# Attention probabilities left undivided until the values leave PSUM, in a hybrid attention and MLP layer

## The chip, the core and the metric

The kernel runs on one core of a Trainium2 chip. The core has five engines that run side by side, each through its own queue of instructions, in order: PE (TensorE, matmuls), ACT (ScalarE), DVE (VectorE), POOL (GpSimd) and SP (SyncE, which here issues every DMA). Matmuls write into PSUM, a memory of eight banks of 128 partitions x 512 f32; everything else lies in SBUF. The metric is device time in microseconds (us).

## What is computed

One layer on 1024 positions of 1024 features. A normalised and modulated x is projected; the columns of the projection feed two groups of eight attention heads, and their outputs go through one output projection; a gated MLP with a short convolution follows. The change concerns only the softmax of the attention heads:

```python
# MLA heads: dense, causal by chunks of 64
s = einsum('bqhd,bkhd->bhqk', q, k) * scale
p = softmax(where(mask, s, NEG_INF))
o = einsum('bhqk,bkhd->bqhd', p, v)
...
# chunk heads: a band of 9 chunks of keys, with a bias by relative position
s = einsum('bqhd,bkhd->bhqk', q, k_band) * scale + bias
p = softmax(where(valid, s, NEG_INF))
o = einsum('bhqk,bkhd->bqhd', p, v_band)
```

## The kernel before

**Stages.** A start (modulation vectors, normalisation, transposes, the first projection) fills the first 95 us. Then the attention runs as one interleaved stream. Its pieces are *units*: one head and one half (g) of the queries, 16 units of chunk attention (names with c) and then 16 of MLA (names with m). A unit has four *tiles* of 128 queries; tile i of a chunk head sees the last five blocks of 128 keys at most, tile i of an MLA head sees i+1 blocks. So a tile's scores are 128 x n with n from 128 to 640 (chunk) or to 1024 (MLA).

**A tile's scores** (`Unit.scores`, L636). PE multiplies the q page by the k pages (L658; each f32 operand is split in a high and a low part, three products for each block) into a two-buffered PSUM tile "S". DVE masks (L665, L676) and takes the row minimum m of the negated scores (L669, L673 or L677). ACT computes exp(m - s) into P and the row sum beside it (L683). DVE takes the reciprocal of the sum and multiplies it by 2^15 (L685, L686): ri, a column of 128. Then the row is split into two f16 halves in "hl": POOL writes the high half, P x ri rounded to f16 (L71, called from L700; all modes are "1"), and DVE writes the low half, P x ri minus the high half (L703). Rows of more than 640 columns go in two pieces, so there are 64 pieces in chunk attention and 88 in MLA. A transposing DMA on SP's queue (L705) turns hl into "PT", keys on partitions. P, hl and PT have three buffers each.

**A tile's values** (`Unit.values`, L709). PE multiplies PT by the f16 values, high and low halves side by side (L716), into the PSUM tile "pv" of the unit, one bank, one buffer. After the fourth tile ACT copies one half of the partitions with a scale (L723), DVE adds the other half, scaled (L724), and SP sends the 64 x 512 result to memory (L725). The scale is a power of two from `pow2_scale` (L337), which also takes the 2^15 out again (L351).

**What sets the order.** The main loop (L817) issues a tile's scores, and values three tiles (DEPTH) later. After each, `pace` takes steps of *fillers*, the projections that the later units need: f_v, f_qk and f_m during chunk attention, f_up (the MLA up-projections; much of it on POOL: L116, L467 to L470, L582) at the change to MLA, and f_oca (part of the output projection, L598 to L611) during MLA. f_ada (L419) streams weights beside them. On top of that a list scheduler orders each engine's queue by priorities: scores may move ahead by 400, the split and transposes by 200, values by 200 (OFF_S, OFF_P, OFF_V). Before a unit starts, its q and k pages are made (`qk_page`, L614): four PE transposes (L618) into a PSUM tile with the tag "T", evicted by ACT (L621 or L624) and DVE (L622 or L625). The tag T has one buffer (TB = 1), one bank; the latents (L496) use it too.

**After the attention** (from about 678 us) come the rest of the output projection, the second normalisation and the MLP. They share no line with the change.

Of the kernel before, what the change touches and what calls it, by code (L numbers as in the profile page):

```python
# [12 lines left out]
F32 = mybir.dt.float32  # L13
# [4 lines left out]
AF = mybir.ActivationFunctionType  # L18
# [3 lines left out]
MUL, ADD, SUB, MIN, MAX = ALU.mult, ALU.add, ALU.subtract, ALU.min, ALU.max  # L22

P = 128
# [14 lines left out]
DEPTH = 3  # L39
OFF_S, OFF_P, OFF_V = 400, 200, 200  # L40
P_BUFS, HL_BUFS, PT_BUFS, TB = 3, 3, 3, 1
MODE_C = "1111"
MODE_M = "1111"
PSCALE, VSCALE = 2.0 ** 15, 2.0 ** 14
R_CA, R_MLA = 1.9, 0.5


# [15 lines left out]
def layer_kernel(ctx, tc, I, out):  # L63
    nc = tc.nc
    pe, act, dve, pool, sp = nc.tensor, nc.scalar, nc.vector, nc.gpsimd, nc.sync
# [4 lines left out]
    def scale_pool(o, i, s):  # L70
        pool.tensor_scalar(o, i, s, 1.0, op0=MUL, op1=MUL)  # L71
# [12 lines left out]
    cst = ctx.enter_context(tc.tile_pool(name="cst", bufs=1))  # L84
# [11 lines left out]
    ident = cst.tile([P, P], F32, name="ident")  # L96
# [33 lines left out]
    ps = psA.__enter__()  # L130
# [105 lines left out]
    for d in range(ND):  # L236
        if d + 1 < ND:
            load_ada(d + 1)
        w = wada[d]
# [15 lines left out]
        for t in range(NT):  # L255
            h, j = divmod(t, 4)
# [80 lines left out]
    def pow2_scale(nm, ssw, b2, n, fac):  # L337
        t = cst.tile([P, 3, ND], F32, name=f"vs{nm}")
        dve.tensor_tensor(t[:, 0, :n], ssw, b2, op=MUL)
        pt = ps.tile([P, 512], F32, name=f"vsp{nm}", tag="mm", bufs=2)  # L340
        pe.matmul(pt[:, :n], ones[:], t[:, 0, :n], start=True, stop=True)
        dve.tensor_reduce(t[:, 1, 0:1], pt[:, :n], axis=AX.X, op=ADD)
        dve.tensor_scalar(t[:, 1, 0:1], t[:, 1, 0:1], fac, 1e-30, op0=MUL, op1=ADD)
        pool.tensor_tensor(t[:, 1, 1:2], t[:, 1, 0:1], nhalf[:], op=ALU.pow)
        ab = cst.tile([P, 2], F32, name=f"vab{nm}")
        dve.tensor_scalar(t[:, 2, 0:1].bitcast(I32), t[:, 1, 1:2].bitcast(I32), 0x7F800000, None, op0=ALU.bitwise_and)
        dve.reciprocal(t[:, 2, 1:2], t[:, 2, 0:1])
        dve.tensor_scalar(t[:, 2, 1:2], t[:, 2, 1:2], 1.0001, None, op0=MUL)
        dve.tensor_scalar(t[:, 2, 1:2].bitcast(I32), t[:, 2, 1:2].bitcast(I32), 0x7F800000, None, op0=ALU.bitwise_and)
        dve.tensor_scalar(ab[:, 0:1], t[:, 2, 0:1], VSCALE, None, op0=MUL)  # L350
        dve.tensor_scalar(ab[:, 1:2], t[:, 2, 1:2], 1.0 / (VSCALE * PSCALE), None, op0=MUL)  # L351
        return ab[:, 0:1], ab[:, 1:2]

    hb = cst.tile([P, ND], F32, name="hb")
# [273 lines left out]
    class Unit:  # L628
# [7 lines left out]
        def scores(u, i):  # L636

            qpg, kpgs = u.pages()
            bias = u.bias() if u.band else None
            lo = max(0, i - 4) if u.band else 0  # L640
            n = (i - lo + 1) * P
            nm = f"{u.nm}_{i}"
            rsum = cst.tile([P, 1], F32, name=f"rs{nm}", tag="rsum", bufs=4)
            ri = cst.tile([P, 1], F32, name=f"ri{nm}", tag="ri", bufs=4)
            with tc.high_priority(offset=OFF_S):
                s = ps.tile([P, 1024], F32, name=f"s{nm}", tag="S", bufs=2)
                n0 = max(0, min(4, i + 1) - lo) * P
                n1 = n - n0
                c0 = 512 - n0 if n1 else 0
                segs = [(c0, lo * P, n0, 0)] if n0 else []  # L650
                if n1:
                    segs.append((512, max(lo, 4) * P - 512, n1, 1))
                q = slice((i % 4) * P, (i % 4 + 1) * P)
                rs_ = slice(u.base, u.base + u.rows)
                for a in range(2):
                    for c, ko, w, kh in segs:
                        for b in range(2 - a):
                            last = pe.matmul(s[:, c:c + w], qpg[rs_, a, q], kpgs[kh][rs_, b, ko:ko + w],  # L658
                                             start=(a == 0 and b == 0), stop=(a == 1))
                trail.append(last.ins)  # L660
                sv = s[:, c0:c0 + n]
                m = cst.tile([P, 1], F32, name=f"m{nm}", tag="m", bufs=4)
                if u.band:
                    if i >= 4:
                        dve.memset(sv[64:128, 0:64], BIG)  # L665
                    w = min(n, 256)
                    if n > 256:
                        m0 = cst.tile([P, 1], F32, name=f"m0{nm}", tag="m0", bufs=4)
                        dve.tensor_reduce(m0[:], sv[:, :n - 256], axis=AX.X, op=MIN)  # L669
                        init = m0[:]  # L670
                    else:
                        init = 3e38
                    dve.tensor_tensor_reduce(sv[:, n - w:n], sv[:, n - w:n], bias[:, 256 - w:256], 1.0, init,  # L673
                                             ADD, MIN, accum_out=m[:])
                else:
                    dve.memset(sv[0:64, n - 64:n], BIG)  # L676
                    dve.tensor_reduce(m[:], sv, axis=AX.X, op=MIN)  # L677
                pieces = [(0, n)] if n <= 640 else [(0, 512), (512, n)]
                if n <= 640:
                    pr = at.tile([P, 640], F32, name=f"P{nm}", tag="P", bufs=P_BUFS)  # L680
                else:
                    pr = pgtile([P, 1024], F32, f"P{nm}")
                act.activation(pr[:, :n], sv, AF.Exp, bias=m[:], scale=-1.0, accum_out=rsum[:, 0:1])  # L683
            with tc.high_priority(offset=OFF_P):
                dve.reciprocal(ri[:], rsum[:, 0:1])  # L685
                dve.tensor_scalar(ri[:], ri[:], PSCALE, None, op0=MUL)  # L686
                u.pt[i] = []
                for x, (p0, p1) in enumerate(pieces):
                    w = p1 - p0
                    hl = at.tile([P, 1280], F16, name=f"hl{nm}_{x}", tag="HL", bufs=HL_BUFS)  # L690
                    pp = pr[:, p0:p1]
                    cnt[0] += 1
                    mode = (MODE_C if u.band else MODE_M)[cnt[0] % 4]
                    if mode == "2":
                        scale_pool(pp, pp, ri[:])
                        act.activation(hl[:, :w], pp, AF.Copy)
                        pool.tensor_tensor(hl[:, w:2 * w], pp, hl[:, :w], op=SUB)
                    else:
                        if mode == "1":
                            scale_pool(hl[:, :w], pp, ri[:])  # L700
                        else:
                            act.activation(hl[:, :w], pp, AF.Copy, scale=ri[:])
                        dve.scalar_tensor_tensor(hl[:, w:2 * w], pp, ri[:], hl[:, :w], op0=MUL, op1=SUB)  # L703
                    tt = at.tile([P, 10, P], F16, name=f"PT{nm}_{x}", tag="PT", bufs=PT_BUFS)
                    sp.dma_start_transpose(tt[:, :2 * w // P, :], hl[:, :2 * w])  # L705
                    u.pt[i].append((tt, lo + p0 // P, w // P))
            return sum(3 * max(107, w / 2.4) for _, _, w, _ in segs)

        def values(u, i):  # L709
            if i % 4 == 0:  # L710
                u.pv = ps.tile([P, 512], F32, name=f"pv{u.nm}_{u.g}", tag="pv", bufs=1)
            c = slice((i % 4) * P, (i % 4 + 1) * P)
            todo = [(lo + j, tt[:, h * nk + j, :]) for tt, lo, nk in u.pt[i] for j in range(nk) for h in range(2)]
            with tc.high_priority(offset=OFF_V):
                for x, (j, mov) in enumerate(todo):
                    last = pe.matmul(u.pv[:, c], u.vst(j), mov, start=(x == 0), stop=(x == len(todo) - 1))  # L716
                trail.append(last.ins)
                if i % 4 == 3:
                    sb = at.tile([P, 512], F32, name=f"sb{u.nm}_{u.g}", tag="sb", bufs=1)
                    dst = at.tile([P, 512], F32, name=f"o{u.nm}_{u.g}", tag="o", bufs=1)  # L720
                    r0, r1 = (slice(64, 128), slice(0, 64)) if u.odd else (slice(0, 64), slice(64, 128))
                    inv = vscale[u.vs][1]
                    act.activation(sb[r0], u.pv[r1], AF.Copy, scale=inv[r1])  # L723
                    dve.scalar_tensor_tensor(dst[r0], u.pv[r0], inv[r0], sb[r0], op0=MUL, op1=ADD)  # L724
                    sp.dma_start(u.dst_d[r0, u.g * 512:(u.g + 1) * 512], dst[r0])  # L725
            return 56 * len(todo)

    cnt = [0]
    biases = {}

    def load_bias(hd):
# [85 lines left out]
    for n in range(len(tiles) + DEPTH):  # L817
        if n < len(tiles):
            u, i = tiles[n]
# [4 lines left out]
        if n >= DEPTH:  # L824
            u, i = tiles[n - DEPTH]
# [326 lines left out]
```

## Time and profile before

| | us |
|---|---|
| median of 3 runs (1463.65 to 1468.99) | 1465.47 |
| the profiled execution | 1464.36 |
| its span, first to last instruction | 1462.2 |
| PE busy over the span | 1278.0 |
| DVE | 1013.6 |
| POOL | 823.0 |
| ACT | 611.4 |

The table of the page gives for each engine its busy time, the share of the span and the number of instructions. PEld is the loading of weights into PE, which overlaps the matmuls. Matmuls are pipelined, and the ends of their records are modelled: the records of neighbours overlap. A row of a group reads: line, engine, operation, what it writes <- what it reads, shapes, xcount | busy us, mean ns of one | idle time of the engine just before, and what ended that wait. A row of waits reads: who waited <- for whom: us in total, times, the longest. PEclk is the clock that was granted to PE, as a share of the full one.

### The profile page before, as it was taken

Reading aid. Unit: us, or ns where it says so; the run is one execution under the profiler, and the core shown is the slowest. Engines: PE = TensorE matmul, PEld = TensorE weight load, DVE = VectorE, ACT = ScalarE, POOL = GpSimd, SP = SyncE. Lnnn points to the kernel's source line nnn. Section 1 sums busy time; section 2 is a strip of 40 time slices with the busy share of each in tenths; the row PEclk is TensorE's granted clock in tenths of the full one; section 3 lists DMA queues with packets and bytes.
Section 4 is the critical chain, followed back from the end, with each engine's and each line's share of the span. In section 5 each row is a group of like instructions: output and inputs, shape, how many; then the busy total and the mean of one; then the engine's idle time right before and its main releaser. Section 6 shows DMA issues by size and latency. Waiting matters only on the chain.

```text
span 1462.2 us, 20198 instructions
## 1 busy us (share of the span) xinstructions
PE 1278.0 (87%) x6836; PEld 1058.7 (72%) x6836; DVE 1013.6 (69%) x1734; ACT 611.4 (42%) x1190; POOL 823.0 (56%) x845
## 2 busy tenths in 40 slices
PE   3859989998967788885776999999999998999997
PEld 2759878886756666664655878788888887887885
DVE  6874776476667868872476887777777777566653
ACT  4453354243455545543274434344444433332331
POOL 5263554274599954534644555566655555665662
PEclk9979987999787899996887999999999999999998
DMA  7323647455522577879611322322222244446442
GB/s 281 134 71 74 131 114 148 129 119 120 112 52 51 115 163 156 180 142 253 246 72 59 105 110 101 116 87 87 87 87 83 75 140 164 151 144 238 146 142 101
DMA packets 218595, 185.94 MB, mean 127 GB/s; under 512 B 148086, under 2 KB 183034, under 8 KB 217468
## 3 DMA queue, kind: packets, MB, share of 16 engines
q1 hardware_dynamic: 218492, 184.66, 44.5%
q8 instruction: 54, 0.88, 0.3%
q14 instruction: 49, 0.40, 0.1%
HBM read 121.17 MB, written 28.84 MB: 103 GB/s over the span
## 4 chain that ended last, share of the span: by engine, by line
PE 39%; DMA 17%; DVE 15%; POOL 13%; issue 12%; ACT 3%; SPq 1%; DVEq 0%; POOLq 0%; ACTq 0%
POOL wds L82 5%; DMA aw<-w_ada 5%; PE p L924 4%; PE p L926 4%; PE p L925 4%; DMA wu<-w_up 3%; DMA PTm<-hlm 3%; PE sc L658 2%; PE dnp L1067 2%; PE dnp L1069 2%; PE dnp L1068 2%; PE sm L658 2%; DVE adacc L243 2%; DVE aacc L430 1%; DVE u L1002 1%
## 5 line engine op out<-in xcount | busy, mean ns | idle before, releaser
L82 POOL TENSOR_TENSOR wds<-wd,wds 128x512 fp32r<-128x512 f32 x88 | 154.6, 1777 | 99.0 <-ACT wds L75 99.0
L82 POOL TENSOR_TENSOR wc<-ws,wc 128x512 fp32r<-128x512 f32 x22 | 65.4, 2972 | 137.8 <-ACT wc L75 137.8
L1057 DVE TENSOR_TENSOR wd<-wd,gmbc 128x1024 f32<-128x1024 f32 x44 | 67.5, 1533 | 80.4 <-DMA wd<-w_down 80.4
L1069 PE MATMUL dnp<-wds,g 128*128 128x512 f32 x308 | 118.4, 390 | 4.5 <-DVE g L82 4.5
L1067 PE MATMUL dnp<-wds,g 128*128 128x512 f32 x308 | 119.6, 390 | 1.9 <-DVE xo L1075 1.9
L75 ACT ACTIVATE wds<-wd 128x512 fp32r<-128x512 f32 x88 | 54.8, 624 | 157.3 <-PE dnp L1069 152.2
L1068 PE MATMUL dnp<-wds,g 128*128 128x512 f32 x308 | 119.5, 389 | 0.0
L71 POOL TENSOR_SCALAR hlm<-Pm,rim 128x512 f16<-128x512 f32 (+4 forms) x88 | 61.9, 706 | 70.1 <-DMA PTm<-hlm 55.1
L703 DVE SCALAR_TENSOR_TENSOR hlm<-Pm,rim,hlm 128x512 f16<-128x512 f32 (+4 forms) x88 | 68.0, 777 | 30.1 <-POOL hlm L71 29.7
L71 POOL TENSOR_SCALAR hlc<-Pc,ric 128x640 f16<-128x640 f32 (+2 forms) x64 | 45.3, 710 | 76.9 <-DVE ric L686 41.2
L1015 DVE TENSOR_TENSOR ws<-wu,wu 128x512 f32<-128x512 f32 x22 | 30.7, 1396 | 76.2 <-DMA wu<-w_up 76.2
L82 DVE TENSOR_TENSOR g<-gr,g 128x512 fp32r<-128x512 f32 x44 | 71.9, 1635 | 11.5 <-ACT g L75 11.5
L1001 DVE SCALAR_TENSOR_TENSOR u<-c,pk,u 128x1023 f32<-128x1023 f32 x44 | 77.4, 1765 | 2.0 <-ACT u L1000 2.0
L1036 ACT ACTIVATE u<-u 128x1024 f32<-128x1024 f32 x22 | 23.4, 1063 | 132.1 <-DVE u L1002 132.1
L683 ACT ACTIVATE Pc<-sc,mc 128x640 f32<-128x640 f32 (+2 forms) x64 | 42.1, 659 | 82.5 <-DVE mc L673 62.0
L658 PE MATMUL sm<-mk,mq 96*128 96x512 f32 (+3 forms) x288 | 68.9, 372 | 7.9 <-ACT Pm L683 7.3
L1000 ACT ACTIVATE u<-c,pk 128x1024 f32<-128x1024 f32 x44 | 52.3, 1236 | 56.2 <-DVE c L1032 56.2
L716 PE MATMUL pvm<-PTm,vt 128*128 128x128 f16 x576 | 50.5, 242 | 28.8 <-DMA PTm<-hlm 24.3
L658 PE MATMUL sc<-k,q 64*128 64x512 f32 (+3 forms) x288 | 70.3, 372 | 4.9 <-ACT Pc L683 3.0
L430 DVE SCALAR_TENSOR_TENSOR aacc<-aw,cs,aacc 128x256 f32<-128x256 f32 x84 | 44.9, 535 | 40.6 <-DMA aw<-w_ada 40.0
L716 PEld LDWEIGHTS <-vt 128*128 128x128 f16 x576 | 41.1, 109 | 41.7 <-issue 38.3
L1069 PEld LDWEIGHTS dnp<-wds,g 128*128 128x128 f32 x308 | 57.8, 188 | 17.7 <-DVE g L82 5.7
(368 smaller groups left out, 4342.0 us busy)
## 6 DMA issues: line engine op xcount, KB each, us to landing
wu<-w_up SPq DMA_DIRECT2D x44, 512.0 KB, 4.3
wd<-w_down SPq DMA_DIRECT2D x44, 512.0 KB, 4.7
aw<-w_ada SPq DMA_DIRECT2D x96, 128.0 KB, 2.3
g_d<-u SPq DMA_DIRECT2D x22, 512.0 KB, 2.6
gr<-g_d SPq DMA_DIRECT2D x44, 256.0 KB, 3.7
x<-x SPq DMA_DIRECT2D x16, 512.0 KB, 8.3
adaw<-w_ada_a SPq DMA_DIRECT2D x8, 1024.0 KB, 5.5
wq_r<-w_qk SPq DMA_DIRECT2D x32, 128.0 KB, 2.6
```

The costliest lines, as they stand in the source:

```text
L71: pool.tensor_scalar(o, i, s, 1.0, op0=MUL, op1=MUL)
L82: (pool if eng == "p" else dve).tensor_tensor(o, i, f32(hi), op=SUB)
L430: dve.scalar_tensor_tensor(acc[:], w[:], cs[:, k:k + 1], acc[:], op0=MUL, op1=ADD)
L658: last = pe.matmul(s[:, c:c + w], qpg[rs_, a, q], kpgs[kh][rs_, b, ko:ko + w], start=(a == 0 and b == 0), stop=(a == 1))
L703: dve.scalar_tensor_tensor(hl[:, w:2 * w], pp, ri[:], hl[:, :w], op0=MUL, op1=SUB)
L716: last = pe.matmul(u.pv[:, c], u.vst(j), mov, start=(x == 0), stop=(x == len(todo) - 1))
L924: pe.matmul(pt, sh, pg[:, 0], start=(k == 0), stop=False)
L1001: dve.scalar_tensor_tensor(u[:, 1:], c[:, :S - 1], pk[:, cv + 1:cv + 2], u[:, 1:], op0=MUL, op1=ADD)
L1057: dve.tensor_tensor(raw[:], raw[:], gmbc[:], op=MUL)
L1067: pe.matmul(pts[t][n], sh, w[n][:, 0], start=(j == 0), stop=False)
L1068: pe.matmul(pts[t][n], sh, w[n][:, 1], start=False, stop=False)
L1069: pe.matmul(pts[t][n], sl, w[n][:, 0], start=False, stop=(j == NF - 1))
```

## The change

The exponentials are no longer divided by their row sum before they are split. The factor 2^15 moves into the exponent: log(2^15) is added to the column m on DVE before the exponential. ACT then writes the high half as a plain copy to f16, and DVE subtracts it from P. The four row sums of a unit lie in one 128 x 4 tile. At the end of the unit one reciprocal takes all four; four products on PE, each with one column of reciprocals repeated 128 times as the stationary operand and the identity as the moving one, put 1/row sum of every query on all partitions, in a PSUM tile with the tag T; and after L724 DVE multiplies the unit's result by it. Everything else keeps its text. (The lines of the changed kernel are 2 lower up to the softmax, and differ from there on.)

```diff
-MODE_C = "1111"
-MODE_M = "1111"
-PSCALE, VSCALE = 2.0 ** 15, 2.0 ** 14
+LOGP, VSCALE = 15 * math.log(2.0), 2.0 ** 14
...
-        dve.tensor_scalar(ab[:, 1:2], t[:, 2, 1:2], 1.0 / (VSCALE * PSCALE), None, op0=MUL)
+        dve.tensor_scalar(ab[:, 1:2], t[:, 2, 1:2], 1.0 / VSCALE, None, op0=MUL)
...
-            rsum = cst.tile([P, 1], F32, name=f"rs{nm}", tag="rsum", bufs=4)
-            ri = cst.tile([P, 1], F32, name=f"ri{nm}", tag="ri", bufs=4)
+            if i % 4 == 0:
+                u.rsum = cst.tile([P, 4], F32, name=f"rs{nm}", tag="rsum", bufs=4)
...
-                act.activation(pr[:, :n], sv, AF.Exp, bias=m[:], scale=-1.0, accum_out=rsum[:, 0:1])
+                dve.tensor_scalar(m[:], m[:], LOGP, None, op0=ADD)
+                act.activation(pr[:, :n], sv, AF.Exp, bias=m[:], scale=-1.0, accum_out=u.rsum[:, i % 4:i % 4 + 1])
...
-                dve.reciprocal(ri[:], rsum[:, 0:1])
-                dve.tensor_scalar(ri[:], ri[:], PSCALE, None, op0=MUL)
...
-                        if mode == "1":
-                            scale_pool(hl[:, :w], pp, ri[:])
-                        else:
-                            act.activation(hl[:, :w], pp, AF.Copy, scale=ri[:])
-                        dve.scalar_tensor_tensor(hl[:, w:2 * w], pp, ri[:], hl[:, :w], op0=MUL, op1=SUB)
+                    act.activation(hl[:, :w], pp, AF.Copy)
+                    dve.tensor_tensor(hl[:, w:2 * w], pp, hl[:, :w], op=SUB)
...
                     inv = vscale[u.vs][1]
+                    ri = cst.tile([P, 4], F32, name=f"ri{u.nm}_{u.g}", tag="ri", bufs=2)
+                    dve.reciprocal(ri[:], u.rsum[:])
+                    rb = ps.tile([P, 512], F32, name=f"rb{u.nm}_{u.g}", tag="T", bufs=TB)
+                    for j in range(4):
+                        pe.matmul(rb[:, j * P:(j + 1) * P], ri[:, j:j + 1].to_broadcast([P, P]), ident[:],
+                                  start=True, stop=True)
                     act.activation(sb[r0], u.pv[r1], AF.Copy, scale=inv[r1])
                     dve.scalar_tensor_tensor(dst[r0], u.pv[r0], inv[r0], sb[r0], op0=MUL, op1=ADD)
+                    dve.tensor_tensor(dst[r0], dst[r0], rb[r0], op=MUL)
                     sp.dma_start(u.dst_d[r0, u.g * 512:(u.g + 1) * 512], dst[r0])
```

More of the change, by code (lines that the diff above doesn't have):

```diff
@@ L691, in scores @@
                     pp = pr[:, p0:p1]
[L692 to L697, printed above, removed]
-                    else:
-                        if mode == "1":
-                            scale_pool(hl[:, :w], pp, ri[:])
-                        else:
-                            act.activation(hl[:, :w], pp, AF.Copy, scale=ri[:])
-                        dve.scalar_tensor_tensor(hl[:, w:2 * w], pp, ri[:], hl[:, :w], op0=MUL, op1=SUB)
+                    act.activation(hl[:, :w], pp, AF.Copy)
+                    dve.tensor_tensor(hl[:, w:2 * w], pp, hl[:, :w], op=SUB)
                     tt = at.tile([P, 10, P], F16, name=f"PT{nm}_{x}", tag="PT", bufs=PT_BUFS)
@@ L722, in values @@
                     inv = vscale[u.vs][1]
+                    ri = cst.tile([P, 4], F32, name=f"ri{u.nm}_{u.g}", tag="ri", bufs=2)
[4 more added lines that the diff above has]
+                                  start=True, stop=True)
                     act.activation(sb[r0], u.pv[r1], AF.Copy, scale=inv[r1])
                     dve.scalar_tensor_tensor(dst[r0], u.pv[r0], inv[r0], sb[r0], op0=MUL, op1=ADD)
+                    dve.tensor_tensor(dst[r0], dst[r0], rb[r0], op=MUL)
                     sp.dma_start(u.dst_d[r0, u.g * 512:(u.g + 1) * 512], dst[r0])
             return 56 * len(todo)
-    cnt = [0]
     biases = {}
```

## The prediction, made before the result was known

> **What bounds the kernel now.** I read the page's busy table and slices first, then the busy time by stage, then the waits inside the attention stages, then single rows for prices.
>
> ```profile
> span 1462.2 us, 20198 instructions
> ...
> PE 1278.0 (87%) x6836; PEld 1058.7 (72%) x6836; DVE 1013.6 (69%) x1734; ACT 611.4 (42%) x1190; POOL 823.0 (56%) x845
> ...
> PE   3859989998967788885776999999999998999997
> ...
> POOL 5263554274599954534644555566655555665662
> ```
>
> The changed lines run only between 95 and 678 us (slices 3 to 19). The later slices (output projection, MLP) keep their code, so I leave their 784 us alone. The busy times by stretch cut the attention into three stages: chunk attention (95 to 410), the MLA up-projections with the first MLA head (410 to 490), the other MLA heads (490 to 678).
>
> ```profile
> core 0: us, PE busy (x) PEld busy (x) DVE busy (x) ACT busy (x) POOL busy (x), PEclk, DMA share, GB/s
> 95.00:410.00 315.00, 295.57 (x2075) 259.81 (x2075) 202.07 (x601) 133.33 (x352) 160.36 (x241) 0.91 0.53 117
> 410.00:490.00 80.00, 55.49 (x287) 44.52 (x288) 59.19 (x155) 43.02 (x108) 75.67 (x145) 0.83 0.25 52
> 490.00:678.00 188.00, 149.55 (x1018) 119.43 (x1017) 136.22 (x324) 89.90 (x187) 99.39 (x123) 0.90 0.75 159
> ```
>
> Each stage has another limit. In the first PE has a matmul in flight for 295.6 of 315 us: what is added to PE there is on the path. In the second POOL is busy for 75.7 of 80. In the third no engine is full (PE 80%, DVE 72%); the waits of 500 to 680 us show what paces it:
>
> ```profile
> POOL hlm L71 <- DMA PTm<-hlm: 55.1, 33, 4.3
> ...
> DVE hlm L703 <- POOL hlm L71: 24.9, 25, 3.3
> PE pvm L716 <- DMA PTm<-hlm: 18.4, 15, 2.5
> ```
>
> POOL waits for an hl buffer that a transposing DMA still reads, DVE for POOL, PE for the transposed tile: a chain per tile (scores, minimum, exponential, split, transpose, values), kept moving by running scores ahead of values.
>
> **What it removes.** POOL loses all 152 L71 scalings:
>
> ```profile
> L71 POOL TENSOR_SCALAR hlm<-Pm,rim 128x512 f16<-128x512 f32 (+4 forms) x88 | 61.9, 706 | 70.1 <-DMA PTm<-hlm 55.1
> L703 DVE SCALAR_TENSOR_TENSOR hlm<-Pm,rim,hlm 128x512 f16<-128x512 f32 (+4 forms) x88 | 68.0, 777 | 30.1 <-POOL hlm L71 29.7
> L71 POOL TENSOR_SCALAR hlc<-Pc,ric 128x640 f16<-128x640 f32 (+2 forms) x64 | 45.3, 710 | 76.9 <-DVE ric L686 41.2
> ```
>
> That is 107 us of POOL: 45.3 in the first stage, where POOL is half idle (worth nothing), 9.3 in the second, where POOL is the limit, 52.6 in the third. DVE loses 128 reciprocals and 128 multiplies of a column (L685, L686: 10.1 + 9.7 + 9.5 + 9.3 = 38.6 us).
>
> **What ACT and DVE get.** ACT makes the high halves: 152 copies. ACT's copies at L75 take 624 ns for 128x512, 523 for x384, 414 for x256, so 0.82 ns an element; 48 x 0.624 + 24 x 0.523 + 24 x 0.414 + 40 x 0.73 + 16 x 0.31 = 87 us. No row has exactly this copy (f32 to f16 inside SBUF); the f16 eviction at L410 takes 470 ns for 256 columns, so up to 97. ACT is at 42 to 54% in these stages and goes to about 55 to 72%: no limit, but each eviction on it can come 0.6 us later. DVE gets 128 column additions (row L686: 0.147 each, 19 us), 32 reciprocals (5 us) and 32 multiplies of 64x512 with one operand in PSUM (L622, 96x512: 0.68 each, 22 us): +46 against -38.6. Its 152 low halves become two-operand subtractions: L1019, 128x512, takes 723 ns where L703 takes 743 in the first stage and 853 in MLA, so 0 to -12 us; I take -4. DVE stays about even, at 64 to 74%.
>
> **The chain of a tile.** Now, at 612 us: the exponential ends at 612.10, its sum is read until 612.19, reciprocal 612.55, multiply 612.74, POOL 612.89 to 613.58, DVE from 613.85: 1.75 us from exponential to low half. Then: sum read 0.19, copy 0.62, so about 0.9, and 0.18 more before the exponential for the addition to m. Gain 0.6 to 0.7 us of some 8.
>
> **What PE gets.** 32 units x 4 products of f32 with a 128-column operand, none in the trace. Nearest rows, at 269 us:
>
> ```profile
> 269.05 0.50 PE L443 MATMUL p_ada<-ones,aacc 128*128 128x1 f32 x4
> 269.42 0.36 PE L152 MATMUL ipv<-wv_s,hT 128*128 128x256 f32 x1
> 269.62 0.28 PE L150 MATMUL ipv<-wv_s,hT 128*128 128x256 f32 x1
> ```
>
> Two f32 products of one column show as four records and push the stream back by about 0.45 us (their neighbours are 0.12 apart): 0.23 a product, all weight loading. At L456 a 256-column f32 product holds the stream 0.43 us (146.70 to 147.25, less the 0.12 of the matmul behind), so 128 columns stream in 0.22. If loading and streaming overlap, a product costs 0.24 and a unit 0.96 us; if not, 0.45 and 1.8. I take 0.96, since these rows overlap loads everywhere, and divide by the granted clock of 0.91: 1.05 a unit, 34 us in all.
>
> **What the products wait for, and who waits for them.** Their PSUM tile has the tag T, one bank, shared with the q and k pages (L616) and the latents (L496). It is taken when the first product is issued and given back only by the last DVE multiply, after the unit's fourth value tile, ACT's L723 and DVE's L724. Until then no page transposes. A product that waits (for the bank, or for DVE's reciprocal) holds back what stands behind it on PE: values, scores of the next tiles, projection matmuls. The new multiply on DVE waits for the products, and behind it stand the next tile's minimum and low half, for which ACT and SP wait; the unit's output DMA leaves 0.7 us later and nothing near waits for it. In the built program the four products of a unit often stand ahead of the values of its third tile, and the next unit's pages, which stood between earlier scores, stand behind the unit's last values. So scores run ahead less: at the first value matmul of a tile, scores of on average 5.0 later MLA tiles had begun before, 2.4 in the changed program (chunk attention 3.1 and 2.3). A MLA head lasts 25 us (L724 at 564.6, 590.1, 615.3, 641.6), a tile 3.1; the chain of about 7.5 us fits into 2.4 tiles with nothing to spare, while at 11 tiles the lead is 0 or 1 (4 before). SP issues the same 152 transposes (1.23 to 1.32 us each); its waits move only with the chain.
>
> **The sum**, against the profiled execution's own 1464.36 us (span 1462.2 and 2.2 around it; the median of the runs is 1465.47, 0.1% off):
> - Chunk attention: 16 units x 1.05 = +17 on a full PE; of the 9.9 us that PE waits here for transposes a shorter chain takes back about 4: +13. Bounds 0 (all in gaps) and +29 (1.8 a unit).
> - 410 to 490: -9.3 of POOL, +2 units of products, +8 of ACT: I take -6. Bounds -9 and 0.
> - Other heads: 14 units x 1.05 = +15; the shorter chain against the lost lead, I take -2: +13. Bounds -10 (lead harmless, waits of PE halved) and +31 (below).
> Together +20: **1484 us**. Its own range is 1474 to 1494.
>
> [...]
>
> **Rivals.**
> 1. *The held bank rules* (slower still). Where a tile's lead is 1 the chain lacks 7.5 - 3.1 = 4.4 us; 7 more such tiles make 31 us in MLA, and heads of about 28 us. For it: one bank, and the order. Against it: PE has the output-projection matmuls of L608 as filler. With half to all of it the time is 1495 to 1512, say 1502.
> 2. *The relief rules* (faster). POOL's 9 us all come off; in MLA half of PE's 18.4 us of waits for transposes goes (9), a fifth of DVE's 24.9 us of waits for POOL comes through to the end (5), and most products sink into PE's waits, 9 us staying. 1464 - 9 - 9 - 5 + 9 = 1450. It decides if DVE and PE both find their gaps in MLA. For it: a low half of 384 columns took 1.63 us at 616.34, beside a POOL subtraction at 616.27, and 0.62 alone. Against it: that POOL row is L82's, which stays. [...]
> 3. *The products fit into gaps.* Matmul rows of 0.28 us start 0.12 apart, so a busy row hides idle slots; if both large stages swallow their products, 17 + 15 us go from the sum, less what the gaps already held: 1464 - 6 + 5, about 1463: no difference.
>
> **How the numbers follow.** Forecast 0.52, rival 1 0.20, rival 2 0.14, rival 3 0.14. 0.5% (7.3 us) is about what a measurement of this kernel tells from no change. Slower: 0.73 (forecast, rival 1, a tail of rival 3); same 0.13; faster 0.14. The range 1456 to 1508 takes in the forecast, rival 3, most of rival 1 and the upper part of rival 2.
>
> **What would show it.** Right: the 95 to 410 stretch longer by 10 to 17 us with the new rows at about 1 us a unit; POOL below 70 of 80 in the up-projections and that stretch shorter; MLA heads of 26 to 27 us, PE rows waiting longer for DVE's multiply through the T bank; later stages unchanged. Wrong: MLA heads under 25 us, products at 0.5 us a unit or above 1.8, an ACT row as the chain's new last wait, or a change after 690 us.

## The result, and the profile after

The changed kernel takes **1538.38 us** (median of 4 runs, 1535.64 to 1541.15) against 1464.56 (4 runs, 1463.57 to 1468.99): 1.0505 times as long, with a 95% interval of 1.0483 to 1.0526. Slower was forecast, but +20 us, not +74. The time lies outside the range of 1456 to 1508. The profiled execution took 1535.64 us.

From the page of the changed kernel, first its span and busy table, then PE and POOL in slices:

```profile
span 1533.6 us, 20576 instructions
...
PE 1323.7 (86%) x7092; PEld 1094.3 (71%) x7092; DVE 1015.7 (66%) x1670; ACT 688.9 (45%) x1342; POOL 715.8 (47%) x693
...
PE   3869989898858876778675899999999999999997
...
POOL 5252341142498610100263556666555655665662
```

The engines' sums moved much as planned: POOL -107 us, DVE +2, ACT +78, PE +46. No sum by itself explains a span that is 71 us longer: ACT, whose sum grew most, is busy for 45% of it. PE's digits 7, 6, 7, 7, 8 in slices 15 to 19 say where to look: these lie in MLA, where the kernel before showed four 8s (slices 15 to 18).

A unit ends with its last DVE operation. This row of the kernel before, and then the one of the changed kernel, give the start of the first and the last such operation for MLA:

```profile
L724 DVE SCALAR_TENSOR_TENSOR om<-pvm,vabm,sbm x16: 662/746/757, 453.0 to 679.5; 64x512 f32<-64x512 f32 x16
```

```profile
L718 DVE TENSOR_TENSOR om<-om,rbm x16: 648/686/692, 472.4 to 753.0; 64x512 f32<-64x512 f32 x16
```

The last unit ends 73.5 us later, and what follows it takes 782.7 us before and 780.6 after: the whole loss lies in the attention, none behind it. In the same traces the last operation of the last chunk unit starts at 410.2 and 447.6, that of the second MLA unit at 488.9 and 502.2. So chunk attention is 37 us longer, the next stage 24 us shorter, and the other MLA heads 250.8 us instead of 190.6: 60 us longer. A head of MLA (two units) takes 35.8 us on average of these seven (32.5 to 39.2) where it took 27.2 (22.0 to 36.3).

The busy times of the changed kernel in these three stages (columns as in the prediction):

```profile
95.00:448.00 353.00, 321.68 (x2251) 282.95 (x2250) 222.81 (x602) 179.22 (x443) 131.21 (x224) 0.91 0.46 106
448.00:503.00 55.00, 37.69 (x227) 30.53 (x228) 41.93 (x106) 36.40 (x90) 47.49 (x87) 0.88 0.33 66
503.00:754.00 251.00, 186.59 (x1154) 148.99 (x1154) 136.13 (x306) 129.28 (x266) 43.91 (x45) 0.84 0.56 122
```

In the third row no engine is full: PE 74% (80% before), DVE 54% (72%), POOL 17% (53%), ACT 52% (48%). PE idles for 64 us, where it idled for 38, and its clock is 0.84 instead of 0.90. A stage that gets longer while no engine comes near full points to a chain or a buffer. The two rows on the new products exclude that they are the whole of it:

```profile
L714 PE MATMUL rbc<-ident,ric 128*128 128x128 f32 x128 | 22.0, 323 | 0.0
L714 PE MATMUL rbm<-ident,rim 128*128 128x128 f32 x128 | 20.1, 304 | 0.5 <-DVE rim L711 0.5
```

A product shows as two records; all 128 products hold PE for 42 us in the records, 1.3 us a unit, and about 1.05 where eight records run in one piece.

**Where the wait sits.** The tag T has one bank. What asks for it gets it in the order in which the program asks: pages of unit u+1, products of unit u, pages of unit u+2. Before, the pages of the next two units could be transposed as soon as their inputs were there. Now the pages of u+2 stand behind unit u's products, which need the last row sum of u and give the bank back only with the last DVE operation of u. PE's timeline of the changed kernel at the end of one MLA unit (start, duration, line, matmul, in brackets what it idled for):

```profile
708.47 1.05 PE L714 MATMUL rbm<-ident,rim 128*128 128x128 f32 x8
...
714.37 0.61 PE L703 MATMUL pvm<-PTm,vt 128*128 128x128 f16 x8 [0.65 <-DMA PTm<-hlm]
717.07 0.80 PE L703 MATMUL pvm<-PTm,vt 128*128 128x128 f16 x6 [2.09 <-DVE mm L681]
718.38 0.80 PE L703 MATMUL pvm<-PTm,vt 128*128 128x128 f16 x6 [0.51 <-DMA PTm<-hlm]
718.97 1.06 PE L616 MATMUL mq_ps<-ident,qn 128*96 128x128 f32 x4
720.71 1.65 PE L656 MATMUL sm<-mk,mq 96*128 96x512 f32 x3 [0.68 <-ACT mq L619]
```

And DVE at the same place:

```profile
716.28 0.73 DVE L717 SCALAR_TENSOR_TENSOR om<-pvm,vabm,sbm 64x512 f32<-64x512 f32 x1
716.94 0.13 DVE L681 TENSOR_SCALAR mm<-mm 128x1 f32<-128x1 f32 x1
717.05 0.68 DVE L718 TENSOR_TENSOR om<-om,rbm 64x512 f32<-64x512 f32 x1
```

The products took the bank at 708.5 and DVE's multiply returned it at 717.7: 9 us for 1 us of work. Only then does the next q page start (718.97), and the scores that need it wait for it (720.71). The q pages' rows, of the kernel before and then of the changed one, say the same for the whole of MLA (at the end of each, the start of the first and of the last transpose):

```profile
L618 PE MATMUL mq_ps<-ident,qn x64: 270/272/451, 410.5 to 629.8; 128*96 128x128 f32 x64
```

```profile
L616 PE MATMUL mq_ps<-ident,qn x64: 270/273/449, 423.7 to 719.6; 128*96 128x128 f32 x64
```

The last q page came 50 us, two heads, ahead of the end of the last unit (680.2); now it comes 34 us ahead (753.7), one head. The traces show the tie unit by unit. For each of the 14 MLA units from the third on, take the time from the end of the unit two before it to the start of its own q page: in the changed kernel the page starts behind that end every time, by 0.1 to 3.1 us; before, it started 23 to 40 us ahead of it in 13 of the 14.

The direct wait is small. In the changed kernel, the page transposes' own list of what PE idled for in front of them has a new entry:

```profile
  DVE om L718: 8.0, 10
```

8 us in ten waits, against a loss of 74. The rest shows under other names, since each later step starts late: PE's waits for transposed tiles in the third stage are 25.0 us (18.9 before), ACT's for the last DVE operation on m, now the addition, 28.6 (16.4 for the minimum before).

### The profile page after: what moved, and what is told of

It reads as the page before. It is cut to its first block, busy times and chain, and to the rows that moved or that the text cites. A ratio compares the mean times of both kernels' runs of the same rounds, so it can differ in the third digit from the quotient of the medians.

```text
span 1533.6 us, 20576 instructions
## 1 busy us (share of the span) xinstructions
PE 1323.7 (86%) x7092; PEld 1094.3 (71%) x7092; DVE 1015.7 (66%) x1670; ACT 688.9 (45%) x1342; POOL 715.8 (47%) x693
## 4 chain that ended last, share of the span: by engine, by line
PE 47%; DMA 16%; DVE 14%; POOL 11%; issue 7%; ACT 3%; SPq 1%; DVEq 0%; POOLq 0%; ACTq 0%
PE p L917 8%; PE p L919 8%; PE p L918 8%; DMA aw<-w_ada 6%; POOL wds L80 5%; DMA PTm<-hlm 4%; PE dnp L1060 2%; PE dnp L1062 2%; PE dnp L1061 2%; PE sm L656 2%; PE sc L656 2%; DVE adacc L241 1%; DVE aacc L428 1%; PE pvm L703 1%; PE ipq L148 1%
## 5 line engine op out<-in xcount | busy, mean ns | idle before, releaser
L703 PE MATMUL pvm<-PTm,vt 128*128 128x128 f16 x576 | 55.5, 248 | 45.6 <-DMA PTm<-hlm 33.7
L656 PE MATMUL sm<-mk,mq 96*128 96x512 f32 (+3 forms) x288 | 75.9, 392 | 21.1 <-ACT Pm L682 10.6
L80 POOL TENSOR_TENSOR cl<-cl,ch 128x512 fp32r<-128x512 f32 x16 | 20.4, 1276 | 157.0 <-ACT ch L73 144.5
L703 PEld LDWEIGHTS <-vt 128*128 128x128 f16 x576 | 44.7, 113 | 60.3 <-issue 57.2
L690 DVE TENSOR_TENSOR hlm<-Pm,hlm 128x512 f16<-128x512 f32 (+4 forms) x88 | 55.4, 637 | 36.0 <-ACT hlm L689 35.4
L994 DVE SCALAR_TENSOR_TENSOR u<-c,pk,u 128x1023 f32<-128x1023 f32 x44 | 77.5, 1767 | 1.7 <-ACT u L993 1.7
L656 PEld LDWEIGHTS sm<-mk,mq 96*128 96x128 f32 x288 | 52.7, 210 | 35.0 <-ACT Pm L682 13.5
L656 PE MATMUL sc<-k,q 64*128 64x256 f32 (+3 forms) x288 | 66.4, 357 | 12.7 <-DVE k L623 5.8
L1008 DVE TENSOR_TENSOR ws<-wu,wu 128x512 f32<-128x512 f32 x22 | 27.3, 1242 | 73.8 <-DMA wu<-w_up 73.8
```

The lines of the kernel that those rows point to most:

```text
L80: (pool if eng == "p" else dve).tensor_tensor(o, i, f32(hi), op=SUB)
L994: dve.scalar_tensor_tensor(u[:, 1:], c[:, :S - 1], pk[:, cv + 1:cv + 2], u[:, 1:], op0=MUL, op1=ADD)
```

## The experiments

**Theory A**, formed from this: the bank's turns decide. The normalisation's tile ties the pages of the next units to the end of the present one. **Rival B**: the products and the multiply cost PE and DVE that much. **Rival C**: the undivided split on ACT and DVE costs it (ACT as a new bound). **Rival D**: the products stand too early in PE's queue and block what is behind them.

Times below are medians; the ratio is to the kernel before on the same chip, with its 95% interval. The chips differ by up to 0.5% (1462.79 to 1469.94 for the kernel before), so differences between kernels of different chips are given by the times and by the ratios, and the ratios count.

**1. No normalisation** (leaves out the division by the row sum). The split stays.

```diff
-ri = cst.tile(...); dve.reciprocal(ri[:], u.rsum[:])
-rb = ps.tile([P, 512], F32, ..., tag="T", bufs=TB)
-for j in range(4): pe.matmul(rb[...], ri[:, j:j + 1].to_broadcast([P, P]), ident[:], ...)
-dve.tensor_tensor(dst[r0], dst[r0], rb[r0], op=MUL)
```

> The changed kernel without the reciprocal, the products and the multiply at a unit's end (it leaves out the division by the row sum); the split by ACT and DVE stays. Theory A (the T bank, held by the products, takes the lead of scores over values away): most of the 74 us goes, 1465 to 1485. Rival B (the copies on ACT, in line with the exponentials, are the cost): the MLA heads stay at 32 us or more, 1500 to 1520, since only the products' own 30 us go.

Measured: 1466.73 us, 0.9982 [0.9956, 1.0009]. Rival C falls: the undivided split alone makes no difference that can be measured, neither loss nor gain. Without the normalisation there is no loss.

**2. Normalisation alone**: the kernel before, plus the four products in T and the multiply, with ones, made out of the row sums, in place of 1/row sum (the old division stays; the four row sums of a unit lie in one tile, as in the changed kernel).

```diff
+dve.tensor_scalar(one[:], one[:], 0.0, 1.0, op0=MUL, op1=ADD)
+rb = ps.tile([P, 512], F32, ..., tag="T", bufs=TB)
+for j in range(4): pe.matmul(rb[...], one[:, j:j + 1].to_broadcast([P, P]), ident[:], ...)
+dve.tensor_tensor(dst[r0], dst[r0], rb[r0], op=MUL)
```

> The kernel before, with its split on POOL and its division, and the other half of the change alone: at the end of a unit a DVE operation makes a 128 x 4 tile of ones out of the unit's row sums, four products put it on all partitions through the T bank, and DVE multiplies by it, so by 1. Theory A: the built order has a lead of 2.6 tiles in MLA like the changed kernel's 2.4, so 1510 to 1540. Rival B: only PE's products and one DVE multiply a unit, 1480 to 1500.

Measured: 1554.21, 1.0563 [1.0486, 1.0639], above the range expected by either. This half alone reproduces the loss, again without rival C.

**3. Products in another bank**: the tag of the projections, two buffers.

```diff
-rb = ps.tile([P, 512], F32, ..., tag="T", bufs=TB)
+rb = ps.tile([P, 512], F32, ..., tag="mm", bufs=2)
```

> The changed kernel, with the products' tile under the tag mm (two banks, those of the projections) in place of T (one bank). The built order has a lead of 4.2 tiles in MLA (2.4 in the changed kernel). Theory A: MLA heads back to 26 to 28 us, 1475 to 1500. Rival B: nothing of ACT's work changes, 1525 to 1545.

Measured: 1484.25 (1479.74 to 1486.32), 1.0096 [1.0032, 1.0160]. The products, their reciprocal and the multiply are all there, and another tag gives back 54 us (60 by the ratios, 51 by the spans, 1533.6 and 1482.5). Rival B is left with the rest: 17.5 us over run 1, known to some 10 us by the two intervals.

**4. Products late**: placed behind the unit's last value matmul, still in T.

```diff
+with tc.issue_after(last.ins):
     for j in range(4): pe.matmul(rb[...], ...)
```

> The changed kernel, with the products of a unit queued on PE behind its last value matmul, still in T. If what costs is that the products are issued early and hold T during the values of two tiles, 1490 to 1515. If it is that T has to be given back once more in every unit, in whatever order (the built lead stays at 2.3 tiles), or the ACT copies, 1525 to 1550.

Measured: 1537.00, 1.0446 [1.0391, 1.0501]. Rival D falls nearly whole: where the products stand in PE's queue is worth 1 us (9 by the ratios).

**5. Early return**: DVE copies the products out of T at once and multiplies from SBUF later.

```diff
+dve.tensor_copy(dst[r0], rb[r0])
-dve.scalar_tensor_tensor(dst[r0], u.pv[r0], inv[r0], sb[r0], op0=MUL, op1=ADD)
-dve.tensor_tensor(dst[r0], dst[r0], rb[r0], op=MUL)
+dve.scalar_tensor_tensor(sb[r0], u.pv[r0], inv[r0], sb[r0], op0=MUL, op1=ADD)
+dve.tensor_tensor(dst[r0], sb[r0], dst[r0], op=MUL)
```

> The changed kernel, products in T, but DVE copies them to SBUF at once and the unit's end multiplies by the copy, so T comes free without waiting for the unit's values. Theory A, sharpened: T is handed out in the program's order (pages of unit u+1, products of u, pages of u+2), and the cost is that it comes back only when unit u has ended. Then most of the loss goes although a copy per unit is added: 1480 to 1505 (the built lead is 3.0 tiles, 5 tiles under 2; 2.4 and 11 in the changed kernel). If any further use of T costs as much, 1530 to 1545.

Measured: 1517.77, 1.0373 [1.0343, 1.0403]: some 20 us back, and not most of it. The picture that the time for which T is *held* is the cost was too narrow. Returned early, T still reaches the pages of u+2 only after the last exponential of u: they now start 0.9 to 9.3 us ahead of the end of u, not 23 to 40. How much of what is left is that turn, and how much the added copies (0.69 us of DVE a unit), this run does not separate; run 9 tests the turn.

**6. Products twice**: run 3 with each product made two times.

```diff
-for j in range(4):
+for j in (0, 1, 2, 3, 0, 1, 2, 3):
```

> Products under mm as in e3, each made twice (128 more f32 products, no more buffers or waits). If the 18 us between e1 and e3 are PE's time in the products, 1498 to 1506; if they are the wait of the unit's end and the multiply on DVE, 1484 to 1490.

Measured: 1501.24, 1.0260 [1.0231, 1.0290]: 17 us over run 3 by the times, 24 by the ratios, 18 by the spans. A second set costs about what the first cost, or more, so most of the first set's 17.5 us goes to the products and not to the multiply: 17 to 24 us over 32 units are 0.53 to 0.75 us a unit, half to seven tenths of the 1.05 that a unit's products hold PE. It is not all PE's own time: PE idled 5.9 us in front of the products until ACT had evicted an output projection tile of the tag mm (L608 of that kernel; 3.4 in run 3).

**7. The tie alone**: the kernel before, with one product of a single column in T and a multiply by it (again with ones).

```diff
+rb = ps.tile([P, 512], F32, ..., tag="T", bufs=TB)
+pe.matmul(rb[:, 0:1], one[:, 0:1].to_broadcast([P, P]), ident[:, 0:1], start=True, stop=True)
+dve.tensor_scalar(dst[r0], dst[r0], rb[r0, 0:1], None, op0=MUL)
```

> The kernel before with the tie alone: at a unit's end a tile of T takes one product of one column (of ones), and DVE multiplies the result by that column; division and split stay as before. PE gets 0.25 us a unit in place of about 1. Theory A, sharpened: the tie makes the loss, 1520 to 1550 (built lead 2.8 tiles, 12 under 2). If the products' PE time or the multiply make it, 1470 to 1485.

Measured: 1550.42, 1.0596 [1.0566, 1.0627]: +88 us. The row of this run's product in MLA, and that of its multiply (ns of one: least, median, most; then first and last start):

```profile
L728 PE MATMUL rbm<-ident,rsm x32: 165/250/353, 477.2 to 753.4; 128*128 128x1 f32 x32
```

```profile
L731 DVE TENSOR_SCALAR om<-om,rbm x16: 405/498/1452, 478.4 to 764.5; 64x512 f32<-64x512 f32 x16
```

Two records of 250 ns on PE and 0.5 us on DVE for each unit, and the loss is larger than that of the whole change (and just above the 1520 to 1550 expected). Rival B is out as the main cause. The changed kernel is 13 us better than this run by the ratios, whose intervals are apart, though it has more work for PE. So the shorter chain of the new split may help while scores run short ahead, which no run tests by itself; run 1 shows that the split is worth nothing that can be measured where they do not.

**8. Half the width**: run 3, the products only on the 64 partitions that the multiply reads.

```diff
-pe.matmul(rb[:, j * P:(j + 1) * P], ri[:, j:j + 1].to_broadcast([P, P]), ident[:],
+pe.matmul(rb[r0, j * P:(j + 1) * P], ri[:, j:j + 1].to_broadcast([P, 64]), ident[:],
```

> e3 with 64 stationary columns in place of 128 (the products fill only the 64 partitions that are read). If weight loading sets a product's price, it falls by up to half: 1475 to 1480. If streaming 128 f32 columns does, no difference from e3: 1482 to 1487.

Measured: 1494.58, 1.0215 [1.0185, 1.0245], 10 us *slower* than run 3 by the times, 17 by the ratios, which nothing expected. The weight loads got shorter (median record 190 to 137 ns), the matmul records did not (275 to 273). Its products wait longer for the tag mm (7.2 us until ACT's eviction L608, 3.4 in run 3), and DVE for them (6.1 us, 2.9); whether that makes the end come later stays open.

**9. Pages first**: the changed kernel, but the main loop asks for a unit's pages one unit earlier, ahead of the products.

```diff
-need(u.need)
-u.prep()
+for v in units[n // 4 + (n > 0):n // 4 + 2]:
+    need(v.need)
+    v.prep()
```

> The changed kernel, T as it is, but the main loop makes a unit's pages one unit earlier, so T is handed to the pages of unit u+2 before the products of unit u. No work is added or taken away. If the order in which the one bank is handed out makes the loss (pages behind the end of a unit), most of it goes: 1480 to 1505 (built lead 3.1 tiles, 4 under 2; 2.4 and 11 in the changed kernel). If it is any holding of T by the products, 1525 to 1545.

Measured: 1491.32, 1.0157 [1.0123, 1.0190]. T keeps its one bank, its products and its late return; only who asks first is changed, and 47 us come back (51 by the ratios). The new entry of above (8.0 us of the page transposes' waits for L718 in MLA) is gone from this run's list, and the q pages start 10 to 17 us ahead of the end of the unit two before. What is left, 1.6%, is about what the products (1.0% in run 3) and the edit itself (0.4%, run 10) cost.

**10. The same edit on the kernel before**, as a control.

> The control: the kernel before with its pages made one unit earlier in the same way. Scores there run 5.0 tiles ahead already (5.05 in this build), so no difference is expected: 1455 to 1475.

Measured: 1474.16, 1.0039 [1.0022, 1.0057]. The edit by itself costs about 6 us, so run 9 gained in spite of it.

**11. The same edit on run 3.**

> e3 (products in mm) with the pages one unit earlier: nothing of T is held by products there, so if the order of T is what matters, no difference from e3, 1475 to 1490.

Measured: 1497.42, 1.0198 [1.0163, 1.0233], 13 us over run 3 (15 by the ratios) and above the range expected. The two cures do not add: once the products are out of T, the pages are ahead already, and the edit only costs, as in the control, where it cost 6; why more here stays open.

**One measure parts these runs.** In PE's order, count the tiles that are scored between an MLA unit's q page and that unit's own first scores (mean over units). Beside it stands the time of above, from the end of the unit two before to the start of the q page (mean of 14 units; minus is ahead of that end):

| run | tiles between page and scores | page after that end, us | ratio |
|---|---|---|---|
| before | 4.6 | -26.6 | 1 |
| 1 no normalisation | 4.6 | -19.3 | 0.998 |
| 10 control | 4.2 | -26.5 | 1.004 |
| 3 products in mm | 4.75 | -31.3 | 1.010 |
| 11 both cures | 4.6 | -35.2 | 1.020 |
| 8 half the width | 4.9 | -33.1 | 1.022 |
| 6 products twice | 3.9 | -30.7 | 1.026 |
| 9 pages first | 1.9 | -13.2 | 1.016 |
| 5 early return | 0.9 | -4.6 | 1.037 |
| 4 products late | 0.6 | 0.9 | 1.045 |
| changed kernel | 0.75 | 1.1 | 1.050 |
| 2 normalisation alone | 0.4 | 1.4 | 1.056 |
| 7 tie alone | 1.0 | 0.9 | 1.060 |

Every kernel with 1.0 or less loses 3.7% or more, every one with 1.9 or more 2.6% or less, and the 2.6% is the run with every product made twice. The second column parts them in the same way: where the page starts behind the end the loss is 4.5 to 6.0%, 4.6 us ahead of it 3.7%, 13 us or more ahead 2.6% or less. The lead of scores over values, which the prediction used, falls too: in MLA it is 3.1 or more in the second group where it was counted (3.1 in run 9, 3.4 in run 1, 4.2 in run 3, 5.0 before) and 3.0 or less in the first (3.0 in run 5, 2.8 in run 7, 2.4 in the changed kernel). So a lead of 2.4 tiles was not enough; but runs 5 and 9, at 3.0 and 3.1, lose 3.7 and 1.6%, so the lead alone does not tell them apart. No count here gives the size of the loss in us.

A second buffer is one way back and not the only one: in run 3 a tag of two buffers gave 54 us back, in run 9 the one bank stayed and 47 us came back.

## Why the prediction was wrong

Direction, removed work and most prices stood; the sum failed in one term. In sizes, +74 is about 51 to 60 for the turn of the bank (changed kernel less run 3), 17 for the products and the multiply (run 3 less run 1), and -3 for the split (run 1, -6 to +1 by its interval).

- **What it removes.** Right: POOL lost 107.2 us of busy time, as counted. Set against the copies on ACT, it was worth nothing by the end: run 1 has all of this relief and stays at 0.998.
- **What ACT and DVE get.** Right in size. An ACT copy of 128x512 takes 628 ns (0.62 forecast), one of 128x640 takes 735 (0.73); ACT has 77.5 us more where 87 was worked out; DVE 2 us more, "about even".
- **The chain of a tile**, 0.6 to 0.7 us shorter. In the changed kernel one tile without waits reads 0.78 us from the end of its exponential (706.98) to its low half (707.76), where about 0.9 was worked out. What it is worth was not measured alone; it had no worth in run 1.
- **What PE gets**, 1.05 a unit. As a holding of PE it is right (1.05 us for the eight records at 708.47). As a cost it was too much, up to twice: the first set cost 17.5 us in all (run 3 less run 1) instead of the sum's 17 + 15 = 32, and a second set 0.53 to 0.75 a unit (run 6).
- **Chunk attention +13, the stage behind it -6.** Measured +37 and -24. Neither stage stands for itself: the last chunk unit waited while the up-projections, fillers of the next stage, went ahead. Together they are +13 where +7 was forecast. Run 3 shows it more strongly: its last chunk unit ends at 466.3, 56 us later than before, and its last MLA unit at 696.9, only 17 later.
- **The step that failed** is the third term, "Other heads: 14 units x 1.05 = +15; the shorter chain against the lost lead, I take -2: +13". It measured +60. I had seen all of it: one bank, returned only by DVE's last multiply, pages moved behind the unit's last values, the lead halved. Then I set the lost lead off against a shorter chain, on the ground that a chain of 7.5 us "fits into 2.4 tiles with nothing to spare". Nothing to spare was the warning. In runs 3 and 9 the same chain with the pages ahead loses 1.0 and 1.6%; without, 5.0%. The 25 us and 3.1 us a tile, with which the chain was compared, were read from the quick heads in the middle; the seven heads took 27.2 on average. And longer heads were not among the signs of being wrong.
- **Rival 1, "the held bank rules"**, had the mechanism, at half its price: heads of about 28 us and 1502, measured 35.8 on average and 1538. (Its 1495 to 1512 cannot be redone from its terms: half to all of 31 us on top of the sum of 1484 gives 1500 to 1515.) Its price counted seven more tiles with a lead of 0 or 1, at 4.4 us. What came late was every unit, since each unit's pages stand behind the end of an earlier one. Its word against, that PE has L608's matmuls as filler, carried little: PE still idled 64 us.
- **Rival 2 (relief) and rival 3 (gaps).** Relief showed nothing in run 1. Of rival 3, a part held: the first set of products cost 17.5 us at the end where the sum put down 32, so PE's gaps can have taken up to half of their time. PE's shares of busy time could not tell this ahead: in chunk attention it had a matmul in flight for 295.6 of 315 us (94%) and a weight load for 259.8 (82%), and what the products cost in that stage alone was not measured.

## What to carry to other kernels

Before adding a tile to a one-buffered PSUM tag, write down who asks for it and in which order: if the new user waits for the end of a piece of work, everything that asks after it, prefetches above all, waits too, and the bank's turn can cost more than the work put into it (here 51 to 60 us against 17). Where a stage grows and no engine comes near full, look at such a turn, and test it by giving the tile another tag or by asking in another order. In an interleaved stream with fillers, price the sum of the stages; one stage alone gives and takes work from the next.

No version here beats the kernel before. The floor for the split is run 1 (0.998) and with the products in another bank it is 1.010, so the undivided split has nothing to pay for its normalisation with.

## What the runs showed of the hardware that was not expected

Between 510 and 670 us (160 us of MLA) the granted clock was lower in the changed kernel and in run 7, in which PE was busy less. The rows of this stretch, of the changed kernel, of the kernel before, of run 7 and of run 3:

```profile
510.00:670.00 160.00, 120.48 (x744) 96.25 (x744) 90.48 (x202) 85.33 (x175) 29.63 (x29) 0.87 0.55 119
```

```profile
510.00:670.00 160.00, 130.43 (x908) 104.39 (x907) 116.59 (x281) 77.89 (x160) 76.72 (x92) 0.94 0.77 161
```

```profile
510.00:670.00 160.00, 117.00 (x677) 90.76 (x676) 93.25 (x226) 62.32 (x128) 69.52 (x88) 0.82 0.55 119
```

```profile
510.00:670.00 160.00, 141.23 (x1007) 116.90 (x1005) 111.75 (x262) 106.75 (x223) 25.77 (x20) 0.93 0.72 152
```

With PE busy for 117.0, 120.5 and 130.4 of 160 us the clock is 0.82, 0.87 and 0.94; in the eight kernels with more than 130 us it is 0.90 to 0.96, in the five with less 0.82 to 0.91. This holds for this stretch and is no rule: in the kernel before, PE was busy for 23.35 us of the first 50 at a clock of 1.00, and for 45.38 us of 200 to 250 at 0.73. The matmul records of this stretch are longer on average in the changed kernel, but not by the median: the first of the three 128x512 products of the output projection (L150, L148 in the changed kernel) takes 432 ns on average before and 480 in the changed kernel, with a median of 395 and 397 and a least of 387 and 388. So part of the +60 in MLA may be slower matmuls; how much, if any, was not separated. In the third stage of the changed kernel (503 to 754 us) PE idles for 64 us at a mean clock of 0.84, and the longest wait listed for it is 3.3 us, for a transposed tile; what sets the clock these runs do not separate.
